# Another order for the 77 block products of an FFN input, on one Trainium2 core

## The chip, the core and the metric

One core of one Trainium2 chip runs the whole kernel in one launch. The metric is the time on the device in microseconds (us); a profile of one execution stands beside it. Engines are named as the profile names them: PE is the matrix engine (PEld its weight load), ACT the scalar engine, DVE the vector engine, POOL the general one, and SP the engine whose queue issues most of the DMAs.

## The reference, cut to what matters

One layer of a decoder: three token mixers, a gated merge, an output projection, then a SwiGLU feed-forward network (FFN) and a last norm, on 512 tokens of width 1024. The change lies in the FFN:

```python
h = h + merged @ w_out
hn = _rmsnorm(h, norm2_w)
a_part, b_part = jnp.split(hn @ w_ffn_in, 2, axis=-1)      # 1024 -> 2 x 2816
return h + (jax.nn.silu(a_part) * b_part) @ w_ffn_out       # 2816 -> 1024
```

All data is float32.

## The kernel before, in words

**Precision.** Every float32 operand of a matmul is split in two pieces of the PE's faster type: `h`, the value rounded (an ACT cast), and `l`, what the rounding left (a DVE subtraction `src - h`). A product takes three matmuls, h·h, h·l and l·h. So each block of weights costs one cast to a `wh` tile, one subtraction into a `wl` tile, and then matmuls. `wh` and `wl` rotate over three buffers each (`wpool`, line 226 on), so the cast for one product can begin only when the product three places earlier has ended.

**The units and the seven products.** The 2816 columns of each half of `w_ffn_in` are cut in 11 units of 256 (`NU = 11`). Unit u is a 2x2 block product: the weights are two loaded tiles, `raws[u][0]` (columns of a_part) and `raws[u][1]` (b_part), each cut in two halves of the 1024-wide contraction (`quarter`); the normed activations are `B11, B21` (tokens 0 to 255, both halves of the contraction) and `B12, B22` (tokens 256 to 511). Instead of eight block products seven are formed, from sums of blocks, as in Winograd's form of Strassen's method. `T1` to `T4` are the sums on the activations' side (`combine_x`, line 1080), once for all units. The sums on the weights' side are formed in place by DVE for each unit (`combine_w`, line 1109; `S1` for product 5). Products are written (u, p), p from 1 to 7.

**Accumulators.** `multiply` (line 1153) sends product (u, p) into one of three accumulators of the unit, each one PSUM bank: r1 takes 1, 6, 7, 4; r2 takes 2; r3 takes 5 and 3. A product is 24 matmuls of 128x128 by 256 columns. The sums on the way are results too, so `collect` (line 1178) takes a copy of r1 by ACT after 1 (`p1`), after 6 (`u2`) and after 7 (`u3`), 128x512 each: the next product into r1 must not begin before that copy is done. After 7, DVE adds r3 and u3 (`cs<-r,u`, the gate), which must be done before 3 goes into r3; after 2 it adds r2 and p1; after 3, r3 and u2; silu on ACT and multiplications on DVE make the two `hid` tiles of the unit.

**The order around the change.** PE runs in the written order; the other engines' queues are ordered by the tile scheduler. The loop near line 1230 walks over `plan`, a list of the 77 products. At place n it forms an activation sum if `XSUMS` says so, prepares place n + 2 (`prepare`, line 1210: its weights are split, and the sums of place n + 3 are issued), multiplies and collects. `prepare` of (u, 3) also issues the loads of unit u + 2 on SP's queue (`load_unit`, line 1102): two DMAs of 1 MB into the buffers of unit u. Units 0 to 2 have special loads (`early_weights`); `ahead_raw[2]` is an extra copy of the a-tile of unit 2.

**What follows.** `token_major` (line 957) multiplies the 22 `hid` tiles with `w_ffn_out`: for k from 0 to 21 it takes `hidden_part(k, ...)`, which casts hid k to `hidh` and subtracts to `hidl` when first asked for, and runs 24 matmuls of 512 columns into eight accumulators. Every split goes through one helper class, so the profile's line for nearly all of them is L90, and groups are told apart by tile names.

Of the kernel before, what the change touches and what calls it, by code (L numbers as in the profile page):

```python
# [9 lines left out]
R32 = mybir.dt.float32r  # L10
# [85 lines left out]
def kernel(  # L96
# [82 lines left out]
    def need(st):  # L179
        while not st.done():  # L180
            if not st.step(force=True):
                clk.pe += 0.2
        if st in streams:
            streams.remove(st)
# [3 lines left out]
    def nm(s):  # L188
        uid[0] += 1
        return f"{s}_{uid[0]}"  # L190
# [4 lines left out]
    def slot(tag, name, dtype=F32, shape=(P, T)):  # L195
        return spool.tile(list(shape), dtype, name=nm(name), tag=tag, bufs=SLOTS[tag])
# [43 lines left out]
    def split(src, h, l):  # L240
        ACT.copy(h, src)
        DVE.tensor_tensor(l, src, h, op=OP.subtract)
# [795 lines left out]
    NU = NH // 2  # L1038
# [5 lines left out]
    def pieces(tag, name, dtype=F32):  # L1044
        return [slot(tag, name, dtype, (P, 2, HW)) for _ in range(2)]
# [34 lines left out]
    def combine_x(name):  # L1080

        b11, b21, b12, b22 = (whole[g, t] for t in range(2) for g in range(2))
        o, x, y = {"T1": (b11, b12, b11), "T2": (b11, b22, b11), "T3": (b12, b22, b12), "T4": (b21, b21, b11),
                   "B22": (b22, None, None)}[name]
        h, l = block(name)[:2]
        for j in range(2):
            if x is not None:
                DVE.tensor_tensor(o[j], x[j], y[j], op=OP.subtract)
            split(o[j], h[j], l[j])

    wfi = w_ffn_in[0]
    raws, ahead_raw, first_sum, parts, res, snap = {}, {}, {}, {}, {}, {}
    gate_, hid = {}, {}

    def load_raw(u, ab, tag):
        rv = (wpool.tile([P, KD, 256], F32, name=nm("raw"), tag="raw", bufs=2) if tag == "raw"
              else slot(tag, "raw", F32, (P, KD, 256)))
        c0 = ab * FH + 256 * u
        SP.dma_start(rv, wfi[:, c0:c0 + 256].rearrange("(k p) n -> p k n", p=P))
        return rv  # L1100

    def load_unit(u):
        if 2 <= u < NU:
            raws[u] = [load_raw(u, ab, "xn" if u % 2 else "raw") for ab in range(2)]

    def quarter(u, i, j):
        return raws[u][i][:, 4 * j:4 * j + 4, :]

    def combine_w(u, p):

        sub = OP.subtract
        if p == 5:
            first_sum[u] = pieces("m", "S1")
            for j in range(2):
                DVE.tensor_tensor(first_sum[u][j], raws[u][1][:, 2 * j:2 * j + 2, :], raws[u][1][:, 4 + 2 * j:6 + 2 * j, :], op=OP.add)
        elif p == 6:
            DVE.tensor_tensor(quarter(u, 1, 0), quarter(u, 0, 0), quarter(u, 1, 0), op=sub)
            for j in range(2):
                a = raws[u][0][:, 2 * j:2 * j + 2, :]
                DVE.tensor_tensor(a, first_sum[u][j], a, op=sub)  # L1120
        elif p == 3:
            DVE.tensor_tensor(quarter(u, 0, 1), quarter(u, 0, 1), quarter(u, 0, 0), op=sub)
# [4 lines left out]
    def weights(u, p):  # L1127
        if (u, p) in parts:
            return
        h = wpool.tile([P, 4, HW], R32, name=nm("wh"), tag="wh")  # L1130
        l = wpool.tile([P, 4, HW], R32, name=nm("wl"), tag="wl")
        if p == 5:
            for j in range(2):
                split(first_sum[u][j], h[:, 2 * j:2 * j + 2, :], l[:, 2 * j:2 * j + 2, :])
        elif u in ahead_raw and p in (1, 2):
            i, j = WHERE[p]
            split(ahead_raw[u][:, 4 * j:4 * j + 4, :], h, l)
        else:
            split(quarter(u, *WHERE[p]), h, l)
        parts[u, p] = (lambda k: h[:, k, :]), (lambda k: l[:, k, :])  # L1140
# [12 lines left out]
    def multiply(u, p):  # L1153
        r, first = {1: (1, True), 6: (1, False), 7: (1, False), 4: (1, False), 2: (2, True), 5: (3, True), 3: (3, False)}[p]
        if first:
            res[u, r] = (pmm if r == 1 else paux)(f"r{r}")
        ps = res[u, r]
        wh, wl = parts.pop((u, p))
        xh, xl = block(RHS[p])[:2]
        for c in range(2):  # L1160
            o = ps[:, c * HW:c * HW + HW]
            for k in range(4):
                a, b = xh[k // 2][:, k % 2, :], xl[k // 2][:, k % 2, :]
                PE.matmul(o, lhsT=wh(k)[:, tsl(c)], rhs=a, start=first and k == 0 and c == 0, stop=False, **G)
                PE.matmul(o, lhsT=wh(k)[:, tsl(c)], rhs=b, start=False, stop=False, **G)
                PE.matmul(o, lhsT=wl(k)[:, tsl(c)], rhs=a, start=False, stop=k == 3 and c == 1, **G)
                tick()
# [10 lines left out]
    def collect(u, p):  # L1178

        if p == 1:  # L1180
            keep(u, "p1")
        elif p == 2:
            a0 = added(u, 2, "p1")
            for c in range(2):
                i = 2 * u + c
                hid[i] = slot("T2" if i < 4 or 8 <= i < 12 else "T1" if i < 8 else "yP" if i < 20 else "A", "hid")
                ACT.activation(hid[i][:, :HW], a0[:, c * HW:c * HW + HW], AF.Silu)
        elif p == 6:
            keep(u, "u2")
        elif p == 7:  # L1190
            keep(u, "u3")
            gate_[u] = added(u, 3, "u3")
        elif p == 4:
            for c in range(2):
                h = hid[2 * u + c][:, :HW]
                DVE.tensor_tensor(h, h, res[u, 1][:, c * HW:c * HW + HW], op=OP.mult)
        elif p == 3:
            a1 = added(u, 3, "u2")
            ACT.activation(a1, a1, AF.Silu)
            for c in range(2):  # L1200
                cs = slice(c * HW, c * HW + HW)
                DVE.tensor_tensor(hid[2 * u + c][:, HW:], a1[:, cs], gate_[u][:, cs], op=OP.mult)

    LEADERS = 3
    plan = [(u, p) for u in range(LEADERS) for p in (1, 2)]
    for u in range(NU):
        plan += [(u, p) for p in ((5, 6, 7, 4, 3) if u < LEADERS else (1, 5, 6, 2, 7, 4, 3))]
    XSUMS = {3: "T1", 4: "T2", 6: "T3", 7: "T4", 8: "B22"}

    def prepare(n):  # L1210
        if n >= len(plan):
            return
        u, p = plan[n]
        weights(u, p)
        if (u, p) == (2, 2):
            raws[1][1] = load_raw(1, 1, "xn")
        if p == 3:
            load_unit(u + 2)
        if n + 1 < len(plan):
            combine_w(*plan[n + 1])  # L1220

    norms2 = []
    token_major(w_out[0], KD, lambda k: mgh[k], lambda k: mgl[k], 3,
                lambda t, a0, a1: norms2.append(start_now(after_out(t, a0, a1))), ahead=early_weights)
    for st in norms2[:2]:
        need(st)
    prepare(0)
    prepare(1)
    for n, (u, p) in enumerate(plan):
        if n == 3:  # L1230
            for st in norms2[2:]:
                need(st)
        if n in XSUMS:
            combine_x(XSUMS[n])
        prepare(n + 2)
        multiply(u, p)
        collect(u, p)
# [3 lines left out]
    for t in range(NT):  # L1241
        for hf in range(2):
            SP.dma_start(xr[t][hf], hrows[t][hf])
    hidden = {}

    def hidden_part(k, part):
        if k not in hidden:
            h, l = slot("A", "hidh", R32), slot("A", "hidl", R32)
            split(hid[k], h, l)
            hidden[k] = h, l  # L1250
        return hidden[k][part]

    of = out[0]

    def after_ffn(t, a0, a1):
        ys = residual(t, a0, a1, fnrow, t == NT - 1)
        for hf in range(2):
            (SP, AQ)[hf].dma_start(of[tsl(t), hf * T:hf * T + T], ys[hf])

    token_major(w_ffn_out[0], NH, lambda k: hidden_part(k, 0), lambda k: hidden_part(k, 1), 3, after_ffn, tag="xn")  # L1260


# [25 lines left out]
```

## Time and profile before

| | us |
|---|---|
| runs shown | 3135.02, 945.59, 943.55; median 945.59 |
| the profiled execution's own time | 945.64 |
| its span, first to last instruction | 943.9 |
| FFN input, first to last product | 564.9 to 813.3 of the span |
| FFN output, first to last matmul | 815.5 to 933.3, then the last norm and stores |

The span is what the timeline counts; 1.7 us of the execution lie around it. A row of the timeline has start, length, engine, line, operation, tiles written and read (buffer numbers left out, so that r1, r2 and r3 all read `r`, p1 reads `p`, u2 and u3 read `u`, T1 to T4 read `T`), and, in brackets, how long the engine was idle before it and whom the profile takes for the releaser. Matmuls overlap: the distance of their starts is what one costs, not their length.

### The profile page before, as it was taken

How to read it: one execution, taken by the hardware profiler on the slowest of the kernel's cores; microseconds unless marked ns; L12 is line 12 of the kernel's file. 1: busy time of each engine (PE TensorE's matmuls, PEld its weight loads, DVE VectorE, ACT ScalarE, POOL GpSimd, SP SyncE). 2: the span in 40 equal slices, each digit the busy share in tenths (PEclk: the TensorE clock that was granted, in tenths of full speed). 3: DMA queues.
4: the chain of work that ended last, by engine and by line, in shares of the span. 5: the costliest groups of instructions: out<-in, count | busy, mean ns of one | idle time of the engine just before them, and what ended most of it. 6: DMA issues, size and time to landing. Idle time of an engine off the chain costs nothing. (4 is left out here: it accounts for less than half of the span.)

```text
span 943.9 us, 12826 instructions
## 1 busy us (share of the span) xinstructions
PE 896.4 (95%) x5121; PEld 774.6 (82%) x5121; DVE 612.4 (65%) x972; ACT 419.9 (44%) x729; POOL 95.6 (10%) x96
## 2 busy tenths in 40 slices
PE   6999899999999999999999999789999999899997
PEld 5887678888888877778888889789999999788885
DVE  6487999955654567676434379877777776533326
ACT  5446333346563345444322279334444444423224
POOL 2060000011111132422000030000000000000001
PEclk9999999999999999999999999999999999999999
DMA  7132112222212211225325331432222224523102
GB/s 236 46 112 90 45 45 90 90 90 90 90 45 82 75 45 57 90 73 166 108 92 199 111 123 57 147 121 91 90 91 90 90 91 144 191 95 120 53 0 90
DMA packets 74318, 90.80 MB, mean 96 GB/s; under 512 B 4297, under 2 KB 63249, under 8 KB 74258
## 3 DMA queue, kind: packets, MB, share of 16 engines
q1 hardware_dynamic: 72578, 87.62, 28.2%
q10 hardware_dynamic: 1680, 2.36, 0.8%
q8 instruction: 40, 0.66, 0.3%
q14 instruction: 20, 0.16, 0.1%
HBM read 85.78 MB, written 4.19 MB: 95 GB/s over the span
## 5 line engine op out<-in xcount | busy, mean ns | idle before, releaser
L90 DVE TENSOR_TENSOR wl<-raw,wh 128x1024 fp32r<-128x1024 f32 (+1 forms) x171 | 207.6, 1214 | 122.7 <-ACT wh L90 118.3
L90 ACT CAST wh<-raw 128x1024 fp32r<-128x1024 f32 (+1 forms) x173 | 174.6, 1009 | 241.4 <-PE mm L90 70.9
L90 PE MATMUL mm<-xnh,wh 128*128 128x512 f32 (+1 forms) x480 | 194.9, 406 | 0.2 <-ACT xnh L90 0.2
L90 PE MATMUL mm<-xnl,wh 128*128 128x512 f32 (+1 forms) x480 | 184.4, 384 | 1.1 <-DVE xnl L90 1.1
L90 PE MATMUL mm<-xnh,wl 128*128 128x512 f32 (+1 forms) x480 | 184.5, 384 | 0.0
L90 PE MATMUL r<-T,wh 128*128 128x256 f32 x704 | 129.5, 285 | 20.8 <-ACT u L90 20.8
L90 PEld LDWEIGHTS r<-T,wh 128*128 128x128 f32 x704 | 109.5, 192 | 23.6 <-ACT u L90 23.6
L90 PEld LDWEIGHTS mm<-xnh,wl 128*128 128x128 f32 x480 | 91.7, 191 | 18.3 <-DVE wl L90 0.3
L90 PEld LDWEIGHTS mm<-xnl,wh 128*128 128x128 f32 x480 | 92.2, 192 | 16.2 <-DVE xnl L90 1.6
L90 PEld LDWEIGHTS mm<-xnh,wh 128*128 128x128 f32 x480 | 92.2, 192 | 15.7 <-issue 1.6
L90 PE MATMUL r<-T,wl 128*128 128x256 f32 x352 | 99.5, 283 | 0.0
L90 PE MATMUL r<-B,wh 128*128 128x256 f32 x464 | 84.4, 283 | 0.0
L90 PEld LDWEIGHTS r<-B,wh 128*128 128x128 f32 x464 | 72.4, 192 | 0.0
L90 PE MATMUL acc<-wh,hidh 128*128 128x512 f32 x176 | 69.1, 392 | 2.1 <-ACT hidh L90 2.1
L90 PE MATMUL acc<-wl,hidh 128*128 128x512 f32 x176 | 69.0, 392 | 0.0
L90 PEld LDWEIGHTS r<-T,wl 128*128 128x128 f32 x352 | 67.5, 192 | 0.0
L90 PE MATMUL r<-B,wl 128*128 128x256 f32 x232 | 65.7, 283 | 0.0
L90 PE MATMUL acc<-wh,hidl 128*128 128x512 f32 x176 | 55.5, 394 | 0.3 <-DVE hidl L90 0.3
L90 DVE TENSOR_TENSOR hidl<-hid,hidh 128x512 fp32r<-128x512 f32 x22 | 14.9, 690 | 55.9 <-ACT hidh L90 53.2
L90 PEld LDWEIGHTS r<-B,wl 128*128 128x128 f32 x232 | 44.5, 192 | 0.0
L90 ACT CAST hidh<-hid 128x512 fp32r<-128x512 f32 x22 | 13.3, 621 | 63.4 <-PE acc L90 63.4
L90 PEld LDWEIGHTS acc<-wh,hidh 128*128 128x128 f32 x176 | 33.4, 190 | 9.3 <-ACT hidh L90 2.3
(260 smaller groups left out, 1422.2 us busy)
## 6 DMA issues: line engine op xcount, KB each, us to landing
raw<-in_w_in_dram SPq DMA_DIRECT2D x26, 1024.0 KB, 5.0
raw<-in_w_ffn_in_dram SPq DMA_DIRECT2D x23, 1024.0 KB, 5.0
raw<-in_w_ffn_out_dram SPq DMA_DIRECT2D x11, 1024.0 KB, 4.9
raw<-in_w_up_ssd_dram SPq DMA_DIRECT2D x4, 1024.0 KB
raw<-in_w_out_dram SPq DMA_DIRECT2D x4, 1024.0 KB, 5.3
xb<-in_x_dram SPq DMA_DIRECT2D x4, 512.0 KB, 4.0
raw<-in_w_in_dram SPq DMA_DIRECT2D x4, 512.0 KB, 5.9
raw<-in_w_up_pool_dram SPq DMA_DIRECT2D x2, 1024.0 KB, 4.9
```

Source lines behind the costliest of these rows:

```text
L90: return fn(*args, **kw)
```

## The change: what it does

The plan was, for units 0 to 2, products 1 and 2 of all three units first and then 5, 6, 7, 4, 3 of each; from unit 3 on 1, 5, 6, 2, 7, 4, 3, unit by unit. Now there is always a product that belongs elsewhere between two that go into one accumulator: the middle of the list repeats (u, 1), (u-1, 4), (u-1, 3), (u, 5), (u, 6), (u, 2), (u, 7). Three smaller edits go with it. `T3` is formed at place 5 instead of 6 (T1 and T2 at places 3 and 4 as before). (2, 2) reads unit 2's regular tile and no longer the extra copy, and the second load of unit 1 is issued with the preparation of (2, 1) instead of (2, 2). The splits of hid 0 and hid 1 for the FFN output are issued at the places 73 and 75 of the list, no longer when `token_major` asks for them.

```diff
-        elif u in ahead_raw and p in (1, 2):
+        elif u in ahead_raw and p == 1:
...
-    LEADERS = 3
-    plan = [(u, p) for u in range(LEADERS) for p in (1, 2)]
-    for u in range(NU):
-        plan += [(u, p) for p in ((5, 6, 7, 4, 3) if u < LEADERS else (1, 5, 6, 2, 7, 4, 3))]
-    XSUMS = {3: "T1", 4: "T2", 6: "T3", 7: "T4", 8: "B22"}
+    plan = [(0, 1), (0, 2), (1, 1), (1, 2), (2, 1), (0, 5), (0, 6), (1, 5), (0, 7), (1, 6), (0, 4), (0, 3), (1, 7),
+            (2, 2), (1, 4), (1, 3), (2, 5), (2, 6), (3, 1), (2, 7), (3, 5), (2, 4), (2, 3), (3, 6), (3, 2), (3, 7)]
+    for u in range(4, NU - 1):
+        plan += [(u, 1), (u - 1, 4), (u - 1, 3), (u, 5), (u, 6), (u, 2), (u, 7)]
+    z = NU - 1
+    plan += [(z, 1), (z - 1, 4), (z, 5), (z, 6), (z - 1, 3), (z, 7), (z, 2), (z, 4), (z, 3)]
+    XSUMS = {3: "T1", 4: "T2", 5: "T3", 7: "T4", 8: "B22"}
...
-        if (u, p) == (2, 2):
+        if (u, p) == (2, 1):
             raws[1][1] = load_raw(1, 1, "xn")
...
+        if n >= len(plan) - 4 and n % 2:
+            hidden_part((n + 4 - len(plan)) // 2, 0)
```

**ACT in the repeating part, unit 4.** Below stands ACT's queue from the copy of r1 after (4, 6) on, with buffer numbers; before, r1 of unit 4 is `r1_1034` and its weights are `raw_992` (a) and `raw_993` (b).

```order
L90 COPY u2_1041_5815<-r1_1034_5731 128x512
L90 CAST wh_1048_5853<-raw_992_5389 128x1024
L90 ACTIVATE hid_1046_5849<-cs_1045_5847 128x256
L90 ACTIVATE hid_1047_5851<-cs_1045_5847 128x256
L90 CAST wh_1054_5889<-raw_1021_5623 128x1024
L90 COPY u3_1052_5885<-r1_1034_5731 128x512
L90 CAST wh_1058_5923<-S1_1056_5893 128x512
```

Now r1 of unit 4 is `r1_1029`, and its weights are `raw_1002` and `raw_1003`; unit 5 has `raw_1025` and `r1_1058`:

```order
L90 COPY u2_1041_5815<-r1_1029_5663 128x512
L90 CAST wh_1048_5852<-raw_1003_5460 128x1024
L90 ACTIVATE hid_1046_5848<-cs_1045_5846 128x256
L90 ACTIVATE hid_1047_5850<-cs_1045_5846 128x256
L90 CAST wh_1052_5885<-raw_1002_5458 128x1024
L90 COPY u3_1050_5881<-r1_1029_5663 128x512
L90 CAST wh_1060_5924<-S1_1056_5893 128x512
L90 COPY p1_1059_5922<-r1_1058_5897 128x512
```

The copies of r1 keep their places behind one cast of weights. What moved is which product the casts belong to: the cast ahead of u3 was for (5, 1) and is now for (4, 3), and p1 of unit 5 follows u3 of unit 4.

**DVE in the repeating part, unit 4.** Before, around the two sums `S1` of unit 5, whose b-tile is `raw_1022`:

```order
L90 TENSOR_TENSOR wl_1030_5690<-S1_1028_5660,wh_1029_5689 128x512
L90 TENSOR_TENSOR S1_1056_5893<-raw_1022_5625 128x512
L90 TENSOR_TENSOR S1_1057_5894<-raw_1022_5625 128x512
L90 TENSOR_TENSOR cs_1031_5722<-r3_1009_5528,u2_1012_5581 128x512
L90 TENSOR_TENSOR wl_1033_5728<-raw_992_5389,wh_1032_5727 128x1024
```

Now, with `raw_1026` the b-tile of unit 5, `wl_1034` the weights of (4, 6), `wl_1037` those of (4, 2) and `wl_1040` those of (4, 7):

```order
L90 TENSOR_TENSOR wl_1034_5726<-raw_1002_5458,wh_1033_5725 128x1024
L90 TENSOR_TENSOR S1_1056_5893<-raw_1026_5657 128x512
L90 TENSOR_TENSOR S1_1057_5894<-raw_1026_5657 128x512
L90 TENSOR_TENSOR cs_1035_5753<-r3_1004_5465,u2_1012_5581 128x512
L90 TENSOR_TENSOR wl_1037_5759<-raw_1002_5458,wh_1036_5758 128x1024
L90 TENSOR_TENSOR hid_1017_5614<-cs_1035_5753,cs_1022_5649 128x256
L90 TENSOR_TENSOR hid_1018_5616<-cs_1035_5753,cs_1022_5649 128x256
L90 TENSOR_TENSOR raw_1002_5458<-raw_1002_5458 128x1024
L90 TENSOR_TENSOR wl_1040_5788<-raw_1003_5460,wh_1039_5787 128x1024
```

The sums of the next unit moved from behind the split of (4, 5) to behind the split of (4, 6). They read the tile that is loaded for unit 5, and the splits for (4, 2) and (4, 7) stand behind them.

**ACT at the end of the FFN input.** Before, from the copy after (10, 7) on; `hidh` tiles are the casts of hid 0, 1 and 2, `wh_1244`, `wh_1248` and `wh_1253` weights of the FFN output:

```order
L90 CAST wh_1244_7370<-raw_1243_7368 128x1024
L90 COPY u3_1222_7281<-r1_1206_7131 128x512
L90 CAST wh_1248_7402<-raw_1243_7368 128x1024
L90 CAST wh_1253_7436<-raw_1252_7434 128x1024
L90 ACTIVATE cs_1224_7335<-cs_1224_7335 128x512
L90 CAST hidh_1246_7374<-hid_907_4800 128x512
L90 CAST hidh_1250_7406<-hid_908_4802 128x512
L90 CAST hidh_1255_7440<-hid_921_4879 128x512
```

And now:

```order
L90 CAST hidh_1214_7217<-hid_907_4800 128x512
L90 ACTIVATE cs_1213_7212<-cs_1213_7212 128x512
L90 CAST wh_1220_7254<-raw_1170_6825 128x1024
L90 COPY u3_1218_7250<-r1_1201_7067 128x512
L90 CAST wh_1248_7378<-raw_1247_7376 128x1024
L90 ACTIVATE hid_1224_7285<-cs_1223_7283 128x256
L90 ACTIVATE hid_1225_7287<-cs_1223_7283 128x256
L90 CAST hidh_1226_7289<-hid_908_4802 128x512
L90 CAST wh_1250_7406<-raw_1247_7376 128x1024
L90 CAST wh_1253_7436<-raw_1252_7434 128x1024
L90 ACTIVATE cs_1228_7343<-cs_1228_7343 128x512
L90 CAST hidh_1255_7440<-hid_921_4884 128x512
```

The casts of hid 0 and hid 1 went ahead of the last silu (`cs_1228`, of (10, 3)) and of the weights' casts around it; hid 2 stayed behind it. `wh_1220` is the weights of (10, 3), the last product.

## What the change will do to the time: the prediction

> **What bounds the kernel now.** I read the page first, then the groups by form and the waits, then the timeline of PE at each idle place, then the other engines' queues there. The page names the engine and where its chain runs:
>
> ```profile
> PE 896.4 (95%) x5121; PEld 774.6 (82%) x5121; DVE 612.4 (65%) x972; ACT 419.9 (44%) x729; POOL 95.6 (10%) x96
> PE r L90 17%; PE acc L90 12%; ACT wh L90 1%; ACT u L90 0%; ACT hid L90 0%; DVE xr L90 0%; DVE rows L90 0%; DVE wl L90 0%; ACT acc L90 0%; ACT rows L90 0%; DVE hid L90 0%; DVE hidl L90 0%; DVE ms L90 0%; ACT rs L90 0%
> ```
>
> PE is busy nearly all the time, so what can be won is the little that it stands idle on the way. Of the page's groups the products into `r` have most of it, and the waits put all of it down to one releaser, the copy `u` of r1:
>
> ```profile
> L90 PE MATMUL r<-T,wh 128*128 128x256 f32 x704 | 129.5, 285 | 20.8 <-ACT u L90 20.8
> PE r L90 <- ACT u L90: 20.8, 14, 1.6
> ```
>
> Fourteen waits: two in each of units 0 to 2 (6 to 7, 7 to 4), one in each of units 3 to 10 (7 to 4). The chain shows the period, start, length, what:
>
> ```profile
> 631.75 18.87 PE r L90 x156
> ...
> 652.13 1.04 ACT wh L90
> 653.17 0.49 ACT u L90
> ...
> 653.71 18.87 PE r L90 x156
> ...
> 807.47 5.91 PE r L90 x47
> ```
>
> From 631.75 to 807.47 there are eight units of 21.965 us. Product 7 ends, ACT casts weights for 1.04, then copies r1 for 0.49, and only then product 4 begins. (The cast's buffer comes free by the same product's end, so it starts together with it and the copy stands behind.) Two places of PE's timeline give the cost of one product and of one stop:
>
> ```profile
> 599.05 0.28 PE L90 MATMUL r<-T,wl 128*128 128x256 f32 x1
> 599.17 0.40 PE L90 MATMUL r<-B,wh 128*128 128x256 f32 x2
> ...
> 602.05 0.40 PE L90 MATMUL r<-T,wh 128*128 128x256 f32 x2
> ...
> 629.92 0.28 PE L90 MATMUL r<-T,wl 128*128 128x256 f32 x1
> 631.75 0.51 PE L90 MATMUL r<-T,wh 128*128 128x256 f32 x2 [1.55 <-ACT u L90]
> 632.09 0.28 PE L90 MATMUL r<-T,wl 128*128 128x256 f32 x1
> ```
>
> From 599.17 to 602.05 a whole product of 24 matmuls takes 2.88, 0.12 each, and it follows a product into another accumulator without a gap. Seven products are 20.16.
>
> **Part 1: the fourteen waits.** A stop costs more than its idle time: the start after 629.92 should be 630.04 and is 631.75 (1.71), and the first pair then takes 0.34 instead of 0.24. That is 1.81, and 21.965 - 20.16 gives the same from the period. Twelve stops have 1.55 to 1.56 idle; two are shorter:
>
> ```profile
> 596.19 0.51 PE L90 MATMUL r<-T,wh 128*128 128x256 f32 x2 [1.12 <-ACT u L90]
> 613.74 0.50 PE L90 MATMUL r<-T,wh 128*128 128x256 f32 x2 [1.08 <-ACT u L90]
> ```
>
> By the same 0.26 on top they cost 1.38 and 1.34. Sum: 12 x 1.81 + 2.7 = 24.4. In the new list there is one product, 2.88, between any two into r1. ACT still casts first and then copies, so the copy ends about 0.1 + 1.04 + 0.49 = 1.6 after the product: 1.2 before it is needed. All 24.4 go, if nothing else comes late.
>
> **Part 2: hid 0 and hid 1 split earlier.** At the end of the FFN input PE stops once more:
>
> ```profile
> 813.19 0.28 PE L90 MATMUL r<-B,wl 128*128 128x256 f32 x1
> 815.53 0.50 PE L90 MATMUL acc<-wh,hidh 128*128 128x512 f32 x1 [2.06 <-ACT hidh L90]
> ...
> 817.02 1.22 PE L90 MATMUL acc<-wh,hidl 128*128 128x512 f32 x2 [0.30 <-DVE hidl L90]
> 818.04 0.63 PE L90 MATMUL acc<-wh,hidh 128*128 128x512 f32 x1
> 818.47 0.63 PE L90 MATMUL acc<-wl,hidh 128*128 128x512 f32 x1
> ...
> 820.45 0.40 PE L90 MATMUL acc<-wh,hidh 128*128 128x512 f32 x1
> 820.69 0.39 PE L90 MATMUL acc<-wl,hidh 128*128 128x512 f32 x1
> 820.91 0.39 PE L90 MATMUL acc<-wh,hidh 128*128 128x512 f32 x1
> ```
>
> It is idle for 2.06, then 0.30, and from 817.0 to 820.4 its matmuls start 0.43 apart instead of 0.23, because the granted clock is halved:
>
> ```profile
> 817.00:819.00 2.00, 1.98 (x5) 1.59 (x6) 2.00 (x4) 0.56 (x2) 0.00 (x0) 0.50 0.11 45
> 821.00:823.00 2.00, 2.00 (x11) 1.65 (x10) 0.00 (x0) 0.07 (x1) 0.00 (x0) 1.00 0.00 0
> ```
>
> Without a stop the first start would be 813.31, and the twelve matmuls before 820.45 would end at 813.31 + 12 x 0.227 = 816.03. The place costs 4.4. Now the casts of hid 0 and 1 wait for nothing of the last product; the weights of the first k are cast when the third product from the end is done, and cast and subtraction (2.3) fit twice in what follows. hid 2, still behind the last silu, is needed two k later, 48 matmuls or 10.9 us. All 4.4 go, the half clock with the idle time. The same splits are done either way, on engines with room, so the move itself costs nothing.
>
> **Part 3: what the new order asks of DVE, ACT and the loads.** Work per unit is unchanged, in a shorter period:
>
> ```profile
> 652.13:674.10 21.97, 16.55 (x21) 1.00 0.29 97
> L90 DVE TENSOR_TENSOR wl<-raw,wh 128x1024 fp32r<-128x1024 f32 x24 | 29.4, 1224 | 16.1 <-ACT wh L90 15.6
> L90 ACT CAST wh<-raw 128x1024 fp32r<-128x1024 f32 x25 | 26.2, 1049 | 36.1 <-issue 23.9 <-PE r L90 12.2
> ```
>
> DVE would be busy 16.55 of 20.16 (82%), with idle time now before its `wl`. Three buffers let the cast for a product start when the third one before it ends, so cast and subtraction, 1.05 + 1.22, have two products, 5.76. DVE's queue decides whether they get them. I count t from the start of (u, 1). The split of (u, 6) ends at 8.1 (its cast cannot start before (u-1, 4) ends at 5.76). Behind it in the queue stand the two S1 sums, which need the second load of unit u+1. If that has landed they and one addition take 3 x 0.6, the split of (u, 2) ends at 11.1 and is needed at 14.6: 3.5 to spare. The gate must be added before (u-1, 3) at 5.76 and is done near 3. So the load is the thing to price:
>
> ```profile
> raw<-in_w_ffn_in_dram SPq DMA_DIRECT2D x23, 1024.0 KB, 5.0
> 499.75:507.50 7.75, 7.75 (x36) 6.39 (x36) 1.90 (x3) 1.54 (x2) 0.00 (x0) 1.00 0.90 311
> 499.75 0.99 SPq L1099 DMA_DIRECT2D raw<-in_w_ffn_in_dram  x2
> ```
>
> A tile takes 5.0 from issue to landing; the pair issued at 499.75, together, moved its 2 MB by about 507.5 (311 GB/s x 7.75 is 2.4 MB, with the start of a third load in it), so the second of two takes at most 7.8 from the first. Before, loads were issued eight products ahead of use; now the second is issued when the split of (u-1, 3) has read its buffer, at t = 2.4, with the first 2.3 ahead of it. It lands at about 8 by the first figure and 10.3 by the worse one, and PE would wait only from 11.6 on. In the first units the same reckoning, with DVE's queue full, starts from this row and from where T1 was ready:
>
> ```profile
> 566.00:599.00 33.00, 32.86 (x46) 1.00 0.32 105
> 571.91 1.22 DVE L90 TENSOR_TENSOR raw<-raw 128x1024 f32<-128x1024 f32 x1
> 573.05 0.68 DVE L90 TENSOR_TENSOR cs<-r,p 128x512 f32<-128x512 f32 x1
> 573.65 1.28 DVE L90 TENSOR_TENSOR whole<-whole,whole 128x512 f32<-128x512 f32 x2
> 577.82 1.29 DVE L90 TENSOR_TENSOR T<-whole,T 128x512 fp32r<-128x512 f32 x2
> ```
>
> T1 is now needed one product earlier, at 581.6, and ends near 579.1. By the starts, a 1024-wide operation holds DVE for 1.14 and a 512-wide one for 0.60. Up to 573.05 the new queue is the old one; from there to the split of (0, 4) it has 28 of the short and 5 of the long kind, 22.5. That split ends at 595.6 and is needed at 596.2, the closest of all; by the same count those of (2, 2) and (2, 6) end 1.5 to 2 early. For the price of the new order I have nothing from below (it has no fewer instructions), and from above the excess by which a load or split might be late: 0.7 in each of eleven units, 8. I take 0, the value nearest to these margins.
>
> **The sum.** 945.64 - 24.4 - 4.4 = 916.8. The profiled execution is as good as the median, 945.59; the faster run shown is 2 lower. No change is what differs by under 2%, 18.9 us, about what a measurement of this kernel can tell: faster means below 926.7, slower above 964.5.
>
> **Rivals.** *A: the wait moves to the weights' splits.* For it: DVE has no pause from 566 to 599, its queue is served in order, and a sum that waits for a load holds the splits behind it. Against it: margins of 1.5 to 3.5 nearly everywhere. If the second loads landed near 12.3, each unit would lose 0.7: 916.8 + 8 = 925. The start alone being late would cost 1 to 3.
>
> *B: the change does not do what it says, the copies still end too late.* Then 24.4 stay and 941.2 results. They would have to end 1.2 later than by the rows above; ACT idles more than half of each unit, so this is thin.
>
> *C, slower: PE pauses at each change of accumulator and loses its clock.* More banks are live and each product is in another one than the last. A half-clock stretch costs what the one at 817 cost, 8 x (0.43 - 0.227) = 1.6. To eat the 28.8 it takes 18 such stretches, and 30 for 2% slower, of some 65 of 3.4 us in the FFN input; half of them, 32, would end at 968. Against it: the change of accumulator at 599.17 has no gap, and fourteen stops of 1.5 did not halve the clock. The Trainium skill states such a case ("TensorE: Matmul & The Clock Gate", section "A second HAM failure mode: psum-queue depth-cycling"): a kernel that cycled through PSUM banks idled briefly between groups so often that the clock swung between half and full. By that page this change would be a bad one; the trace so far does not bear it out.
>
> **How the numbers follow.** Forecast 0.80 (915 to 922, all faster); A 0.13 (921 to 931, half of it below 926.7); B 0.04 (no difference); C 0.03 (two thirds of it slower). Faster: 0.80 + 0.06 = 0.86; slower 0.02; within 2% the other 0.12. The range: 914.5 below (2 under the sum, as runs differ) and 925 above, which takes in the 8 of the dearest split bound and leaves out half of A, B and C.
>
> **What would show it.** Right: the wait of `r` on `u` is gone from PE's list, the repeating unit takes 20.2, the first `acc` of the FFN output starts 0.1 to 0.2 after the last `r`, and no granted clock of 0.50 stands between them. Rival A shows as PE idle before `r` released by DVE `wl`, with DVE waiting for `raw`; B as `u` waits that remain; C as clocks of 0.50 between 565 and 790. I would be wrong at the root if the units took 20.2 and the time did not fall: something later would then have set the end.

## The result, and the profile after

The changed kernel takes 915.8 us in the median of four executions, the kernel before, run beside it, 944.57. The gain is 28.8 us, as forecast, and the time is 1.0 below the forecast of 916.8. One execution of each kernel was disturbed, 2262.58 us now and 3135.02 before: the medians count it, and without it the times are 914.86 to 916.59 and 943.44 to 945.59, with medians 28.5 apart and a ratio of 0.9696 (95% interval 0.967 to 0.9722). The profiled execution took 914.86, with a span of 913.2.

The page's first part, the same group of products that led before, and from the waits the row of DVE that Part 3 was about:

```profile
PE 888.3 (97%) x5121; PEld 770.6 (84%) x5121; DVE 609.2 (67%) x972; ACT 420.2 (46%) x729; POOL 96.4 (11%) x96
L90 PE MATMUL r<-T,wh 128*128 128x256 f32 x704 | 127.9, 283 | 0.0
DVE S L90 <- DMA raw<-in_w_ffn_in_dram: 7.4, 7, 1.6
```

The idle time before the `r` products, 20.8 before, is 0.0, and the wait of `r` on `u` is gone from PE's list. The chain of waits (start, length, what) ends in two unbroken pieces:

```profile
571.11 216.00 PE r L90 x1800
787.10 115.42 PE acc L90 x509
```

Between 571 and 902 nothing but PE stands on the chain. PE's timeline at the end of the FFN input:

```profile
786.58 0.40 PE L90 MATMUL r<-B,wh 128*128 128x256 f32 x2
786.82 0.28 PE L90 MATMUL r<-B,wl 128*128 128x256 f32 x1
786.94 0.40 PE L90 MATMUL acc<-wh,hidh 128*128 128x512 f32 x1
787.17 0.40 PE L90 MATMUL acc<-wl,hidh 128*128 128x512 f32 x1
```

The first `acc` starts 0.12 after the last `r`, and the next ones 0.23 apart; 2.06 idle and a half clock stood there. One unit as a stretch of the profile (length, then busy time and instructions of PE, PEld, DVE, ACT, POOL, then the granted clock, which is the share of its full clock that PE was given, the DMA share and GB/s):

```profile
640.06:660.22 20.16, 20.16 (x170) 20.16 (x169) 17.29 (x24) 9.75 (x14) 0.00 (x0) 1.00 0.31 106
```

PE is busy for all of 20.16, the seven products of 2.88. From the first product of the FFN input to the first `acc` 224.0 us pass now (562.93 to 786.94) and 250.6 passed before (564.91 to 815.53): the 26.6 less are the 24.4 of the stops and 2.2 at the first `acc`. So the changed place did what was forecast. The two profiled executions, though, differ by 945.64 - 914.86 = 30.8, which is 2.0 more. These 2.0 lie ahead of the FFN input, which begins 1.98 earlier. A part of them is a stretch at half clock 450 us ahead of the change. The same 3.41 us in the kernel before and after, in that order:

```profile
113.68:117.09 3.41, 3.41 (x11) 2.74 (x10) 2.62 (x7) 1.38 (x3) 0.00 (x0) 0.50 0.00 0
```

```profile
113.68:117.09 3.41, 3.41 (x19) 2.88 (x19) 3.34 (x9) 1.11 (x2) 0.00 (x0) 1.00 0.00 0
```

PE did 11 matmuls there before and 19 after. Counted by the same matmul, the kernel before is 0.8 late already at 106.6, 2.1 at 123.1 and 1.7 at 165.2; the 0.8 arose in the first 24 us, and from what is not shown. Of the twelve profiles of this study, four have that stretch (before, and the first, fourth and fifth kernel below). All four begin the FFN input with the old list, but of the eight without it two do so as well (the third and the sixth). Runs without a profile speak for a thing that comes and goes: the changed kernel's 916.59 has a mean granted clock of 0.997 where its 914.86 and 915.01 have 0.999, and one such stretch takes off 0.5 x 3.41 / 915 = 0.002. So I take it to be no part of the change. The runs of one kernel differ by about as much (943.44 to 945.59 before, 914.86 to 916.59 after).

### The profile page after: what moved, and what is told of

Its sections match the earlier page's. It is cut to its first block, busy times and chain, and to the rows that moved or that the text cites. A ratio compares the mean times of both kernels' runs of the same rounds, so it can differ in the third digit from the quotient of the medians.

```text
span 913.2 us, 12813 instructions
## 1 busy us (share of the span) xinstructions
PE 888.3 (97%) x5121; PEld 770.6 (84%) x5121; DVE 609.2 (67%) x972; ACT 420.2 (46%) x729; POOL 96.4 (11%) x96
## 4 chain that ended last, share of the span: by engine, by line
PE 81%; DVE 11%; ACT 3%; issue 2%; POOL 1%; DMA 1%; SPq 0%; ACTq 0%; POOLq 0%; DVEq 0%
PE mm L90 27%; PE r L90 24%; PE acc L90 15%; PE up L90 8%; DVE work L90 2%; DVE wl L90 2%; DVE top L90 2%; PE yatt L90 2%; PE ptr L90 1%; PE yd L90 1%; PE logit L90 1%; POOL win L90 1%; PE yo L90 1%; DVE qT L90 1%; DVE ms L90 1%
## 5 line engine op out<-in xcount | busy, mean ns | idle before, releaser
L90 POOL TENSOR_TENSOR rows<-xr,fnrow 128x512 f32<-128x512 f32 x3 | 3.9, 1295 | 335.1 <-DVE xr L90 335.1
```

The lines of the kernel that those rows point to most:

```text
L90: return fn(*args, **kw)
```

## The experiments

Each ran three rounds beside the kernel before, in three groups, each on one chip: experiments 1 to 4, with 945.56 for the kernel before, 5 and 7 to 9, with 945.84, and 6 and 10, with 944.39. The changed kernel ran in none of them. What is said below against its 915.8 compares across groups, which differ by up to 1.5.

**1. The early splits alone.** The old list; hid 0 and hid 1 are split where the change splits them.

```diff
+        if n >= len(plan) - 4 and n % 2:
+            hidden_part((n + 4 - len(plan)) // 2, 0)
```

> The old order of the products, with only the early splits of hid 0 and hid 1. Theory (the place at the end of the FFN input cost 4.4 by itself, 2.4 of idle time and 1.6 to 1.7 of half clock, the rest restarts): about 940.2 where the kernel before takes 944.6, the fourteen waits of r on u stay at 20.8, and no half clock near the first acc. Rival (the half clock has another cause, for instance the load of FFN-output weights at that time): only 2.4 to 2.8 are won and a clock of 0.50 stays there. Rival (part 2 was worth nothing and the order did all): no change.

Measured: 940.97 (939.42 to 941.98) against 945.56, ratio 0.9948 (0.9931 to 0.9964), so 4.6 less. From its waits, and from PE's timeline after the last `r` at 813.86:

```profile
PE r L90 <- ACT u L90: 20.8, 14, 1.6
```

```profile
813.98 0.40 PE L90 MATMUL acc<-wh,hidh 128*128 128x512 f32 x1
```

The fourteen waits are all there; the stop and the half clock at the first `acc` are gone. Part 2 stands by itself, at 4.6 for 4.4.

**2. The new order alone.** The new list, without the two lines of experiment 1.

> The new order without the early splits of hid 0 and hid 1. Theory: it gains the 24.4 of the fourteen waits and not the 4.4, so about 920.2, with one idle place of about 2 before the first acc; the half clock after it comes or not, as the place falls against the clock's own intervals of 3.4, so 918.5 to 920.5. Rival (the whole difference is the order): 915.8.

Measured: 919.88 (919.46 to 920.89), ratio 0.9731 (0.9717 to 0.9746): 4.1 above the changed kernel. PE's timeline and two stretches:

```profile
789.79 0.50 PE L90 MATMUL acc<-wh,hidh 128*128 128x512 f32 x1 [2.10 <-ACT hidh L90]
...
791.29 1.22 PE L90 MATMUL acc<-wh,hidl 128*128 128x512 f32 x2 [0.30 <-DVE hidl L90]
```

```profile
787.88:791.29 3.41, 1.20 (x5) 0.68 (x5) 3.10 (x6) 3.41 (x7) 0.00 (x0) 1.00 0.83 287
791.29:794.70 3.41, 3.41 (x8) 2.73 (x9) 2.35 (x4) 0.53 (x2) 0.00 (x0) 0.50 0.34 137
```

The stop returns with its half clock, and no `r` waits for `u`. The order is worth 945.56 - 919.88 = 25.7, the splits 4.1 to 4.6; the parts add up.

**3. Old order, copy ahead of cast.** ACT issues the copy of r1 before the cast that stood ahead of it.

```diff
-        ACT.copy(snap[u, name], res[u, 1])
+        copied[0] = ACT.copy(snap[u, name], res[u, 1]).ins
...
-        ACT.copy(h, src)
+        if copied[0] is None:
             ACT.copy(h, src)
+        else:
+            with tc.issue_after(copied[0]):
+                ACT.copy(h, src)
```

> The old order of the products; on ACT each copy of r1 now stands ahead of the cast of weights that used to go before it. Theory (a stop was cast 0.95 and copy 0.58 one behind the other, plus 0.28 of start and restart): the fourteen stops fall from 1.55 idle to about 0.6 and to 0.86 us each in all, 12 to 13 are won, about 932. Rival (PE waits for the copy alone and the cast ahead of it was hidden): no change, 944.6. Rival (the cast, now later, holds up the next product instead): under 5 won, with idle time of PE before wh or wl.

Measured: 934.1 (933.4 to 935.0), ratio 0.9881 (0.9866 to 0.9895), 11.5 less than before. One stop, on PE and on ACT:

```profile
647.27 0.50 PE L90 MATMUL r<-T,wh 128*128 128x256 f32 x2 [0.68 <-ACT u L90]
```

```profile
646.63 0.58 ACT L90 COPY u<-r 128x512 f32<-128x512 f32 x1 [1.28 <-PE r L90]
647.12 1.05 ACT L90 CAST wh<-raw 128x1024 fp32r<-128x1024 f32 x1
```

With the copy first, PE idles 0.67 or 0.68 in thirteen of the fourteen places. Eleven of them had 1.55 or 1.56 and two had 1.12 and 1.08 (the last place, in unit 10, keeps 1.55): 11 x 0.87 + 0.45 + 0.41 = 10.4, of 11.5 measured (9.9 to 12.7 by the interval). So the 1.55 was cast and copy in line, and with the copy alone an `r` still waits. In the old order this edit halves the stop and does not remove it.

**4. The old list for the first three units.** Units 0 to 2 as before, the new list from unit 3 on, with the early splits.

```diff
+    plan = [(u, p) for u in range(3) for p in (1, 2)]
+    plan += [(u, p) for u in range(3) for p in (5, 6, 7, 4, 3)]
+    plan += [(3, p) for p in (1, 5, 6, 2, 7)]
```

> The old list for units 0 to 2 and the new one from unit 3 on, with the early splits of hid. Theory (each stop has its own price): six stops come back, four of 1.81 and two of 1.36, so 10.0 above the changed kernel, about 925.8, with 9 us of waits of r on u. Rival (the new start has costs of its own that the trace hides): less than 8 above.

Measured: 926.35 (925.78 to 927.36), ratio 0.9799 (0.9785 to 0.9814), 10.5 above the changed kernel.

```profile
PE r L90 <- ACT u L90: 8.4, 6, 1.6
```

Six of the fourteen waits, those of units 0 to 2, stay. By the prediction's prices they cost 4 x 1.81 + 1.38 + 1.34 = 10.0. This run also takes back the three small edits at the start (`T3`, the tile of (2, 2), the second load of unit 1); nothing beyond the noise is left for them.

**5. Before, with longer copies.** In the kernel before, each copy of r into its snapshot is done three times (here) or twice (experiment 6).

```diff
-        ACT.copy(snap[u, name], res[u, 1])
+        for _ in range(3):
+            ACT.copy(snap[u, name], res[u, 1])
```

> The kernel before, with each copy of a unit's first partial sum r into u done three times over on ScalarE, which adds two copies of 0.48 us (the step from one copy's start to the next), 0.96 us, before the product that waits can start. Theory (in the old order the copy ends last at each of the fourteen stops, so TensorE pays for it in full): 14 x 0.96 = 13.4 us more, 958 to 959 us. Rival (the stop is set by something else that ends near it, the copy is only the last by a little): less than 4 us more, under 949 us.

Measured: 986.48 (984.77 to 986.72), ratio 1.0428 (1.0411 to 1.0445): 40.6 more, three times what the theory said. From its waits, and two stretches at one stop:

```profile
PE r L90 <- ACT u L90: 39.7, 15, 2.8
```

```profile
667.21:670.62 3.41, 0.67 (x6) 0.47 (x5) 1.94 (x3) 2.70 (x4) 0.00 (x0) 1.00 1.04 359
670.62:674.04 3.42, 3.42 (x18) 3.42 (x18) 2.47 (x4) 0.00 (x0) 0.00 (x0) 0.50 0.23 78
```

The stops grew from 1.83 to 3.02, 0.6 for each copy added (repeated copies start 0.61 apart, not 0.48), the two short ones by 1.6: 17.4 in all. A fifteenth stop of 1.7 came. The other 21 or so are a new loss, which the stops brought: after twelve of them the clock is halved for 3.41, twice for two such lengths. A product's matmuls then start 0.213 apart instead of 0.12, which loses 1.5 each time; 14 x 1.5 = 21. The direction and the place of the theory hold, its size doesn't: it had no price for the clock.

**6. Before, with each copy done twice.** To see from what length a stop takes the clock down.

> The kernel before, with each copy of r into u done twice on ScalarE. In the run with three copies a stop grew from 1.83 to 3.02 us, 0.6 for each copy added, and stretches of 3.4 us at half clock stood behind most of the stops. Theory (each copy on the path costs 0.6 us; a stop of 2.1 us idle alone does not take the clock down, since 3.4 us at half clock stood before only where 2.4 us or more were idle close together): 14 x 0.6 = 8.4 us more, 953 to 955 us. Rival (stops of 2.1 us already halve the clock, 1.7 us a time): up to 14 x 1.7 = 24 us more than that, 965 us or above.

Measured: 969.2 (969.18 to 969.7) against 944.39, ratio 1.0267 (1.025 to 1.0284): 24.8 more, so the rival is right. From its waits, and the stretches at two stops of the same 2.12 idle, that before 758.89 and that before 805.45:

```profile
PE r L90 <- ACT u L90: 29.7, 14, 2.2
```

```profile
755.19:758.61 3.42, 1.57 (x14) 1.37 (x12) 1.77 (x2) 2.18 (x4) 0.00 (x0) 1.00 1.04 355
758.61:762.02 3.41, 3.13 (x26) 3.13 (x27) 2.18 (x4) 0.30 (x2) 0.00 (x0) 1.00 0.62 214
803.00:806.40 3.40, 1.28 (x11) 1.07 (x10) 2.08 (x3) 2.12 (x3) 0.00 (x0) 1.00 1.02 382
806.40:809.81 3.41, 3.41 (x19) 3.41 (x18) 0.95 (x2) 0.00 (x0) 0.00 (x0) 0.50 0.17 70
```

The clock's stretches lie on a grid of 3.413 us (the last section works it out). The first stop straddles a line of the grid, 1.85 idle before it and 0.28 behind, and the clock stays; the second lies within one interval, and the next one is at half. Eleven of the fourteen stops were followed by half clock: 29.7 - 20.8 = 8.9 for the longer stops and 11 x 1.5 for the clock is 25.4.

**7. After, with longer copies.** The changed kernel, three copies each, in the same words as experiment 5.

> The changed kernel, with each copy of r into u done three times over, 0.96 us more per copy. Theory (in the new order another unit's product of 2.88 us stands between a product and the next that overwrites the same accumulator; the copy ends about 1.6 us into it, so 0.96 us more still ends before it): no change, 915 to 917 us. Rival (the copy's end still sets the path somewhere): 10 us more or above, over 925 us.

Measured: 921.15 (920.93 to 921.66), ratio 0.9742 (0.9726 to 0.9759), 5.3 above the changed kernel: between the two. A steady unit on ACT and on PE, then PE at the one place that stops:

```profile
657.25 1.05 ACT L90 CAST wh<-raw 128x1024 fp32r<-128x1024 f32 x1 [1.88 <-PE r L90]
658.20 1.82 ACT L90 COPY u<-r 128x512 f32<-128x512 f32 x3
```

```profile
660.07 0.50 PE L90 MATMUL r<-T,wh 128*128 128x256 f32 x2
...
781.35 0.50 PE L90 MATMUL r<-T,wh 128*128 128x256 f32 x2 [1.50 <-ACT u L90]
```

In the unit the third copy ends at 660.02, 1.24 later than one would, and the product starts at 660.07, 0.07 after its turn: the margin is 1.2 within 0.1. At 781.35 the third copy stands behind a cast that waits for the end of another product, which costs 1.7. That is not all: this profile is 6.2 above the changed kernel's. 2.6 more are delays of 0.1 to 0.2 each, 1.1 stands at 584, where PE waits for DVE's part of `T`, and 0.8 this profile is late before the FFN input begins.

**8. After, with five copies.**

> The changed kernel, with each copy of r into u done five times over, 1.92 us more per copy. Theory (a margin of about 1.2 us between the copy's end and the next product on that accumulator): the copies end 3.5 us after the product, 0.7 late, 0.9 with the restart, at the some 20 places where the two products of one unit have a single product between them: 15 to 22 us more, 931 to 938 us, and waits of r for ACT u come back with about 0.7 us each. Rival (the margin is larger than 2 us): no change, under 919 us.

Measured: 971.33 (967.9 to 973.34), ratio 1.0268 (1.024 to 1.0295), 55.5 above the changed kernel. PE's stop at 655.95 is 1.96 idle, and ACT's timeline has the reason:

```profile
PE r L90 <- ACT u L90: 40.4, 21, 4.0
```

```profile
652.03 2.44 ACT L90 COPY u<-r 128x512 f32<-128x512 f32 x4
654.36 1.05 ACT L90 CAST wh<-raw 128x1024 fp32r<-128x1024 f32 x1
655.31 0.59 ACT L90 COPY u<-r 128x512 f32<-128x512 f32 x1
```

The waits came back at 21 places, as the theory said, but at 1.4 to 2.2 each in nineteen of them and at 3.5 and 4.0 in two, not 0.7: here the fifth copy is queued behind a cast. I had counted only the copies' own time. (Four half-clock stretches add 6, and the restarts, at the prediction's 0.26, some 5.) That the margin is below 2 us holds; its size is better read from experiment 7.

**9 and 10. Later weight loads.** The changed kernel; the second load of each unit from the third on (9), or both (10, without `ab and`), in pieces of half the columns.

```diff
-        SP.dma_start(rv, wfi[:, c0:c0 + 256].rearrange("(k p) n -> p k n", p=P))
+        step = 128 if ab and u > 1 else 256
+        for o in range(0, 256, step):
+            SP.dma_start(rv[:, :, o:o + step], wfi[:, c0 + o:c0 + o + step].rearrange("(k p) n -> p k n", p=P))
```

> The changed kernel, with the second weight load of each unit from the third on written as two loads of 128 columns each in place of one of 256, so that it lands later by some amount d that the trace will give. Theory (from the profile of the changed kernel: in the steady unit the last split that hangs on this load ends 1.8 us before TensorE needs it): TensorE waits d - 1.8 us per unit where d is above 1.8, in eight units, 0 to 20 us more, and the wait shows as r waiting for wl. Rival (VectorE's other work, not the load, sets when the split ends, or the margin is larger): d above 3 us and no change in time.

> The changed kernel, with both weight loads of each unit from the third on written as two loads of 128 columns each. With the second one alone in two, the last split that hangs on it ended about 1 us later and TensorE lost nothing. Theory (its margin is 1.8 us): with the first load in two as well the second lands later still; where the split comes more than 1.8 us later than in the changed kernel, TensorE waits for the rest, 0 to 2 us in each of six units, 916 to 930 us, and the wait is r for wl. Rival (the second load does not get later by having the first in two, or its margin is larger): no wait of r for wl, 915 to 918 us.

Measured: 917.16 (916.58 to 918.18), ratio 0.97 (0.9684 to 0.9715), and 917.3 (916.33 to 918.29), ratio 0.9716 (0.9701 to 0.9731): about 1.4 above the changed kernel, of which the profiles lose 1.3 and 0.6 before the FFN input. DVE's row at the wait of unit 4, in the first:

```profile
652.16 1.29 DVE L90 TENSOR_TENSOR S<-raw 128x512 f32<-128x512 f32 x2 [2.54 <-DMA raw<-in_w_ffn_in_dram]
```

It waits 2.54 for the load where the changed kernel waits 1.60, so the load does set when the split ends. Counted from the unit's start, the splits of units 4 to 9 come 0.5 to 1.6 later in the two runs, with 0.7 or more still to spare. PE has no wait for `wl`; in the first run it loses 0.6 in the whole FFN input and shows one gap of 0.09. That agrees with the changed kernel's margins of 1.8 to 3.3 there, but no load came late enough to cross them: what happens beyond was not tried. In the second, one late load reached PE by another way, seen on DVE, ACT and PE:

```profile
633.71 0.69 DVE L90 TENSOR_TENSOR S<-raw 128x512 f32<-128x512 f32 x1 [2.15 <-DMA raw<-in_w_ffn_in_dram]
...
635.45 0.68 DVE L90 TENSOR_TENSOR cs<-r,u 128x512 f32<-128x512 f32 x1
```

```profile
636.17 0.63 ACT L90 ACTIVATE cs<-cs 128x512 f32<-128x512 f32 x1 [2.99 <-DVE cs L90]
636.71 1.03 ACT L90 CAST wh<-raw 128x1024 fp32r<-128x1024 f32 x1
637.64 0.58 ACT L90 COPY u<-r 128x512 f32<-128x512 f32 x1
```

```profile
638.27 0.51 PE L90 MATMUL r<-T,wh 128*128 128x256 f32 x2 [0.30 <-ACT u L90]
```

The gate's sum stood behind the load's wait on DVE, the silu behind the sum, the cast and the copy behind the silu, and PE lost 0.46. So a late load can use up the copy's margin too.

## Why the prediction was right, step by step

**Part 1, the fourteen waits: right in place and size.** The order alone gained 25.7 (experiment 2) and the difference between experiment 1 and the changed kernel is 25.2, for 24.4. The steps hold singly: the unit takes 20.16; six of the waits cost 10.5 for 10.0; cast and copy in line are what made the stop (experiment 3). The copy's new place, on ACT, ahead of the product that needs it, on PE:

```profile
640.25 1.04 ACT L90 CAST wh<-raw 128x1024 fp32r<-128x1024 f32 x1
641.18 0.58 ACT L90 COPY u<-r 128x512 f32<-128x512 f32 x1
```

```profile
642.94 0.40 PE L90 MATMUL r<-T,wh 128*128 128x256 f32 x2
```

The product into r1 was followed by another at 640.06; the copy ends at 641.76, 1.7 later (1.6 forecast), and 1.2 before 642.94. Experiment 7 measured that 1.2 by using it up.

**Part 2, the early splits: right.** 4.6 and 4.1 for 4.4, with and without the old order.

**Part 3, the price of the new order: 0 was right, but the way there was partly wrong.** The start came as reckoned. The split of (0, 4), the closest of all, was to end 0.6 before need:

```profile
592.50 1.22 DVE L90 TENSOR_TENSOR wl<-raw,wh 128x1024 fp32r<-128x1024 f32 x1
```

It ends at 593.72, its product starts at 593.98 and first reads it 0.24 later: 0.5. The steady unit was tighter than I said. The second load of unit 5, and what stood behind it on DVE:

```profile
643.08 0.37 SPq L1099 DMA_DIRECT2D raw<-in_w_ffn_in_dram  x1
```

```profile
649.85 1.29 DVE L90 TENSOR_TENSOR S<-raw 128x512 f32<-128x512 f32 x2 [1.60 <-DMA raw<-in_w_ffn_in_dram]
651.06 0.68 DVE L90 TENSOR_TENSOR cs<-r,u 128x512 f32<-128x512 f32 x1
651.66 1.21 DVE L90 TENSOR_TENSOR wl<-raw,wh 128x1024 fp32r<-128x1024 f32 x1
```

From the unit's start at 640.06 the load was issued at t = 3.0 (2.4 forecast) and had landed by 9.8 (8 by the first figure, 10.3 by the worse one), 6.8 after its issue. I had taken the 5.0 of a load by itself for one that follows another by 2.3. The split of (4, 2) ended at 12.8, not 11.1, which leaves 1.8 to the 14.6 at which it is needed, not 3.5. DVE's work came out as reckoned: over the five units from 640.06 on it is busy for 16.75 of 20.16 in the mean, 83% for 82% (the 17.29 of the first has operations of its neighbours in it).

**The sum and the profiles.** 28.8 was forecast and measured between medians. That these agree to a tenth is in part luck, as the runs of one kernel differ by 2. The traces bear the sum out better: 26.6 up to the first `acc`, and the twelve matmuls from there on take 2.75 (786.94 to 789.69) where they took 4.92, 2.2 more, which makes 28.8. The time came out 1.0 below the forecast because the profiled execution before, from which the sum starts, was 1.07 above the median. The profiled executions show 30.8; the 2.0 more arose before the FFN input began, in part by the half clock at 113 that one of them had.

**The rivals.** A: no wait for splits in the FFN input, with 1.8 or more left in units 4 to 9; splits later by up to 1.6 do not bring it about, and the one wait that a late load brought came by the copy. B: the copies end in time. C: the clock is 1.00 from 563 to 910, through 77 products that change accumulator each time, so nothing here bears out what the Trainium skill ("TensorE: Matmul & The Clock Gate", section "A second HAM failure mode: psum-queue depth-cycling") has on products that go round the PSUM banks. What took the clock down in these runs were stops: by the last section, rival C's pauses would have had to fill more than half of an interval.

## What to carry to other kernels

Where an engine reads out an accumulator before the next product may overwrite it, put a product into another accumulator between the two, and reckon the read-out with all that stands ahead of it in its engine's queue, here a cast of 1.05 before a copy of 0.5. A margin found for one buffer is used by others too: price a load by the loads around it, and follow each queue from the late item to its end. Before adding a wait to a kernel that keeps PE busy, ask whether it fills more than half of 3.4 us: if so, and if it falls within one interval of the clock, its price here was the wait and 1.5 to 1.7 more.

## What the runs showed of the hardware

The granted clock works on a grid of 3.413 us that stands differently in each execution. In the profile before, the half-clock stretches of 3.41 begin at 113.68 and 816.82, 703.14 or 206 x 3.4133 apart, and in each of the other profiles too all changes of the clock lie whole multiples of it apart. In the twelve profiles each interval at full clock in which PE was idle for 1.86 or more was followed by one at half clock, and none with 1.85 or less was, but for one of 1.72 at the first `acc` of experiment 5. (Gaps above 0.02 are counted, from some 20 us on, where the record of the clock begins; the last us of the programs are left out. Two intervals at half clock, with 0.73 and 0.75 idle, were also followed by another.) So the fourteen stops of 1.55 never cost a clock and those of 2.12 mostly did. It would also explain why the stretch at 113 comes and goes: the changed kernel has a stop of 1.85 that ends at 112.63, as the kernel before has one of 1.86 that ends at 113.43, but a line of its grid parts it into 0.93 and 0.92. The Trainium skill ("TensorE: Matmul & The Clock Gate", section "Part 1: The HAM clock gate (the "warmup" mystery)") has the free-running window of 3413 ns, which the 3.413 here bears out, and the half clock after an idle window of that length; here a window that was idle for 54% was enough, and the measurement decides.
